# Full-width shapes for a few odd products in a two-layer hybrid decoder trunk

## The chip, the cores and the metric

The kernel runs on one core of a Trainium2 chip. The metric is the device time of one execution in microseconds, as the median of several runs. A core has a matrix engine (TensorE, PE in the profile; its weight loads have a row of their own, PEld), a vector engine (VectorE, DVE), a scalar engine (ScalarE, ACT), a general engine (GpSimd, POOL) and an engine that issues transfers (SyncE, SP). All of them run their own instruction streams and wait for each other by semaphores. Matrix results land in PSUM and are moved from there to SBUF by ScalarE or VectorE.

## What is computed

512 tokens and 16 learned ones (528 rows of 1024 features) go through two layers. Cut to what matters:

```python
def reference(x, meta_tokens, ...):
    h = concatenate([meta, x], axis=1)                     # 528 x 1024
    for i in range(2):
        m = _mixer(_rmsnorm(h, pre_mix_norm[i]), ...)
        h = h + _rmsnorm(m, post_mix_norm[i])
        f = _conv_ffn(_rmsnorm(h, pre_ffn_norm[i]), ...)
        h = h + _rmsnorm(f, post_ffn_norm[i])
    return h[:, 16:]

def _mixer(h, ...):
    rq, rk, rv, rg, gq, gk, gv, gr, ga = split(h @ w_in)   # ga: 16 columns, the rank projection
    o_ret = group_norm(retention(rope(rq), rope(rk), rv)) * silu(rg)        # 4 heads
    log_a = log_sigmoid(ga @ gla_gate_w2 + gla_gate_b) / 16
    o_gla = rms_norm(gated_linear_attention(gq, gk, gv, log_a)) * silu(gr)  # 4 heads
    return concatenate([o_ret, o_gla]) @ w_out

def _conv_ffn(h, ...):
    a, g = split(causal_conv3(h @ ffn_up))
    return (gelu(a) * g) @ ffn_down
```

## The kernel before

Features stand on the 128 partitions, tokens along the free dimension. The 528 tokens are cut in two halves for the projections, 0 to 232 and 232 to 528 (`SPLIT`), and in chunks of 128, 128, 128, 128 and 16 (`CHUNKS`) for attention. Each large product runs in f16 as three matmuls per block of 128 features (`product`, L282 to L284): weights and inputs are split in a high and a low f16 part, and high x high, high x low and low x high are summed. A weight block is loaded as f32 (tile `st`), and ScalarE (L86) and VectorE (L87) make its two parts (tile `unit`); `fetch` does that ten blocks ahead. Small products (scores, states, norms, transposes) run in f32, two PE instructions each, a transpose in one.

The rank projection (`project_rank`, L445) has 16 weight columns. Its unit holds high and low part side by side, twice, 64 columns in all, so two matmuls per block of features do (one for each part of the input), and the sum over the parts falls to the following product with `w2`, in which the gate weights are repeated to match. ScalarE and VectorE fill each of the two copies on their own (the loop in `fetch`). `gate_logits` (L607) multiplies rows 0 to 31 and 32 to 63 of that result with `w2`, first for tokens 0 to 232, then for the rest.

Retention handles four blocks of 128 tokens and a last one of 16: `ret_scores` multiplies 16 key columns with 16 query columns (L565, tile `rst`), masks them (tile `dgrt`), and `head_out` multiplies them with the last 16 rows of v (L499), after the product of the 16 queries with the state (L497), into the same PSUM tile.

A norm over features needs a sum over partitions: `token_rstd` multiplies squares with a column of ones (L230, `nst`), takes the power -1/2 on GpSimd (L215), and spreads the result over the partitions by a diagonal (L236 on VectorE, `ndg`) times ones (L237, `nbc`). It does so in equal groups of at most 128 tokens: two for the first half, four of 74 for the 296 tokens of the second.

The first input is normed otherwise, token by token before its transpose. `start` does so for the first two chunks. For the others, `first_xh` takes squares per row, scales the rows (L378, tile `yt`), transposes them (L361) and evicts them as high and low part, on ScalarE (L363) and VectorE (L364). Apart from that, `raw_h` transposes the unscaled rows (L394) and ScalarE copies them (L395) into the residual `h`.

The order of the work has two sources. `start` fixes the order of ScalarE, VectorE and SyncE by hand. All else is put in order by a planner, which places each engine's instructions by costs of its own; the program only gives the dependencies and a rough order: `mixer` runs the projections of the first seven tiles (`LEAD`) on the first half, then on the second, then tile by tile, and after each one it takes two steps (`tick`) of the background generators in `bg`: the first input's second part (`self.later`), gains, constants, raw transposes and the heads. At layer 1's start, and between mixer and feed-forward part, the norms of the second half run while PE works on the first.

Of the kernel before, what the change touches and what calls it, by code (L numbers as in the profile page):

```python
# [14 lines left out]
P = 128  # L15
# [45 lines left out]
class Block:  # L61
# [10 lines left out]
    def fetch(self):  # L72
        if self.unit is not None:
            return
        nc = self.kern.nc
        if self.st is None:
            self.load()
        st = self.st
        if self.w < 64:
            self.unit = self.kern.wpool.tile([P, self.nk, 2, 2, self.w], F16, tag="unit", name="unit")  # L80
            us = [self.unit[:, :, j].rearrange("p k i c -> p i k c") for j in range(2)]
        else:
            self.unit = self.kern.wpool.tile([P, 2, self.nk, self.w], F16, tag="unit", name="unit")
            us = [self.unit]
        for u in us:
            nc.scalar.activation(u[:, 0], st, AF.Copy, scale=SW)  # L86
            nc.vector.scalar_tensor_tensor(out=u[:, 1], in0=st, scalar=SW, in1=u[:, 0], op0=ALU.mult, op1=ALU.subtract)  # L87


class Kern:  # L90
# [105 lines left out]
    def tables(self):  # L196
# [3 lines left out]
        self.tri = self.g([P, P], F32, "tri")  # L200
# [21 lines left out]
    def token_rstd(self, acc, n0, n1, out):  # L222
# [6 lines left out]
        for i in range(nk):  # L229
            nc.tensor.matmul(st[:w, i : i + 1], acc[:, i * w : (i + 1) * w], self.ones[:, :1], start=True, stop=True)  # L230
# [3 lines left out]
        for i in range(nk):  # L234
# [15 lines left out]
    def norms(self, m, acc, xh, n0, n1, rpost, rpre):  # L250
# [18 lines left out]
        bc = out[1]  # L269
        for k in range(KD):  # L270
            t = self.sm([P, WN], "tmp")
            nc.vector.scalar_tensor_tensor(out=t[:, :n], in0=self.h[:, k, n0:n1], scalar=self.pars[:, rpre + k : rpre + k + 1],
                                           in1=bc[:, :n], op0=ALU.mult, op1=ALU.mult)
            self.split(xh[k], t[:, :n], n0, n1)
# [92 lines left out]
    def first_xh(self, t0, t1, n0, n1):  # L367

        nc = self.nc
        ys = []  # L370
        for t in range(t0, t1):
            w = CHUNKS[t][1]
            y = [self.g([P, 512], F32, "yt") for _ in range(2)]
# [653 lines left out]
```

## Time and profile before

| | us |
|---|---|
| median of 3 runs | 1290.46 (1289.42 to 1291.12) |
| the profiled execution, whole | 1289.08 |
| its span, first to last instruction | 1287.3 |
| mean granted clock of TensorE, share of full speed | 0.993 |
| PE busy in the span | 1259.2 |
| VectorE busy | 738.2 |
| ScalarE busy | 605.6 |
| GpSimd busy | 169.2 |

Times inside the profile count from the span's start. An engine is busy while at least one of its instructions is under way. The chain that ended last is followed back from the last instruction, at each step to what released it.

### The profile page before, as it was taken

What the parts mean: (1) busy time and instruction counts of PE and PEld (TensorE: products, weight loads), DVE (VectorE), ACT (ScalarE), POOL (GpSimd) and SP (SyncE); (2) the same over time, 40 slices, a digit from 0 to 9 for tenths busy, and PEclk for the clock granted to TensorE, in tenths of its full rate; (3) what the DMA queues carried; (4) which work ended last, traced back from release to release, by engine and by line L of the source; (5) the groups of instructions that cost most, each with busy time, mean ns of one, the idle gap of its engine ahead of it and who ended that gap; (6) DMA issues with size and microseconds to landing.
All of it is one profiled execution on the core that took longest, in us unless ns stands there. A gap on an engine that the chain in (4) does not pass through costs nothing.

```text
span 1287.3 us, 26505 instructions
## 1 busy us (share of the span) xinstructions
PE 1259.2 (98%) x11198; PEld 1022.3 (79%) x11198; DVE 738.2 (57%) x1408; ACT 605.6 (47%) x1165; POOL 169.2 (13%) x256
## 2 busy tenths in 40 slices
PE   8999999999999999999989999999999999999997
PEld 7687888879888888989876778889788888884443
DVE  6478846357876665431475888453769666664211
ACT  6664434354755555432345544443548555553200
POOL 1023210153000000000340223001420000000000
PEclk9999999999999999999998999999999999999999
DMA  9521221231533343232232222221405333223001
GB/s 257 162 83 51 67 76 57 67 99 34 148 115 99 94 125 90 68 102 70 80 106 83 83 67 66 67 66 51 132 11 172 100 105 108 99 99 131 33 19 48
DMA packets 202171, 115.46 MB, mean 90 GB/s; under 512 B 6256, under 2 KB 193700, under 8 KB 202052
## 3 DMA queue, kind: packets, MB, share of 16 engines
q1 hardware_dynamic: 201892, 113.24, 30.0%
q8 instruction: 87, 1.43, 0.4%
q0 software_dynamic: 160, 0.52, 0.1%
q14 instruction: 32, 0.26, 0.1%
HBM read 111.65 MB, written 2.10 MB: 88 GB/s over the span
## 4 chain that ended last, share of the span: by engine, by line
PE 86%; DVE 6%; ACT 3%; POOL 2%; issue 1%; DMA 1%; SPq 1%; DVEq 0%; POOLq 0%; ACTq 0%
PE pu L283 12%; PE pu L284 12%; PE pu L282 12%; PE pj L283 6%; PE pj L282 6%; PE pj L284 6%; PE pd L283 3%; PE pd L284 3%; PE pd L282 3%; PE pl L921 3%; PE pl L919 3%; PE pl L920 3%; PE po L282 2%; PE po L283 2%; PE po L284 2%; DVE unit L87 1%
## 5 line engine op out<-in xcount | busy, mean ns | idle before, releaser
L87 DVE SCALAR_TENSOR_TENSOR unit<-st,unit 128x1024 f16<-128x1024 f32 (+2 forms) x210 | 254.4, 1215 | 304.3 <-ACT unit L86 303.5
L283 PE MATMUL pu<-xh,unit 128*128 128x296 f16 (+2 forms) x1408 | 384.6, 274 | 1.4 <-DVE xh L220 1.4
L284 PE MATMUL pu<-xh,unit 128*128 128x296 f16 (+2 forms) x1408 | 384.8, 274 | 0.0
L282 PE MATMUL pu<-xh,unit 128*128 128x296 f16 (+2 forms) x1408 | 382.7, 274 | 1.1 <-ACT xh L219 1.0
L282 PEld LDWEIGHTS <-unit 128*128 128x128 f16 x2912 | 285.5, 98 | 48.4 <-issue 5.7
L283 PEld LDWEIGHTS <-unit 128*128 128x128 f16 x2912 | 285.7, 98 | 48.0 <-issue 6.5
L284 PEld LDWEIGHTS <-unit 128*128 128x128 f16 x2912 | 285.8, 98 | 44.8 <-issue 3.1
L86 ACT ACTIVATE unit<-st 128x1024 f16<-128x1024 f32 (+2 forms) x210 | 214.7, 1027 | 110.5 <-PE pl L921 38.9
L282 PE MATMUL pj<-xh,unit 128*128 128x296 f16 (+2 forms) x896 | 247.4, 277 | 2.6 <-DVE on L530 1.6
L283 PE MATMUL pj<-xh,unit 128*128 128x296 f16 (+2 forms) x896 | 247.8, 277 | 0.0
L284 PE MATMUL pj<-xh,unit 128*128 128x296 f16 (+2 forms) x896 | 247.5, 277 | 0.0
L838 ACT ACTIVATE u<-pu 128x296 f32<-128x296 f32 (+2 forms) x176 | 66.9, 382 | 175.4 <-PE pu L284 175.4
L283 PE MATMUL pd<-ffa,unit 128*128 128x296 f16 (+1 forms) x352 | 96.8, 276 | 0.0
L282 PE MATMUL pd<-ffa,unit 128*128 128x296 f16 (+1 forms) x352 | 96.8, 276 | 0.0
L284 PE MATMUL pd<-ffa,unit 128*128 128x296 f16 (+1 forms) x352 | 96.6, 276 | 0.0
L215 POOL TENSOR_TENSOR rs_r<-rs_t,mhalf 128x1 f32<-128x1 f32 (+5 forms) x33 | 39.1, 1189 | 322.6 <-DVE rs_t L214 201.7
L284 PE MATMUL po<-merged,unit 128*128 128x296 f16 (+2 forms) x256 | 69.9, 274 | 0.0
L283 PE MATMUL po<-merged,unit 128*128 128x296 f16 (+2 forms) x256 | 69.9, 274 | 0.0
L282 PE MATMUL po<-merged,unit 128*128 128x296 f16 (+2 forms) x256 | 69.6, 274 | 0.0
L824 DVE SCALAR_TENSOR_TENSOR ca<-u,cvec,ca 128x528 f32<-128x528 f32 (+1 forms) x88 | 66.5, 756 | 1.2
L824 DVE SCALAR_TENSOR_TENSOR cg<-u,cvec,cg 128x528 f32<-128x528 f32 (+1 forms) x88 | 66.3, 753 | 1.2 <-ACT cg L821 1.2
L920 PE MATMUL pl<-unit,ffa 128*128 128x512 f16 x176 | 66.7, 379 | 0.0
(193 smaller groups left out, 1431.0 us busy)
## 6 DMA issues: line engine op xcount, KB each, us to landing
st<-in_ffn_up SPq DMA_DIRECT2D x88, 512.0 KB, 3.8
st<-in_w_in SPq DMA_DIRECT2D x56, 512.0 KB, 3.7
st<-in_ffn_down SPq DMA_DIRECT2D x38, 512.0 KB, 3.8
st<-in_w_out SPq DMA_DIRECT2D x16, 512.0 KB, 3.6
st<-in_ffn_down SPq DMA_DIRECT2D x8, 384.0 KB, 3.4
out<-yo SPq DMA_DIRECT2D x8, 256.0 KB, 2.1
xt<-in_x SPq DMA_DIRECT2D x6, 256.0 KB, 4.4
cosT<-in_c_cos SPq DMA_DIRECT2D x2, 264.0 KB, 7.7
```

The lines of the kernel that those rows point to most:

```text
L86: nc.scalar.activation(u[:, 0], st, AF.Copy, scale=SW)
L87: nc.vector.scalar_tensor_tensor(out=u[:, 1], in0=st, scalar=SW, in1=u[:, 0], op0=ALU.mult, op1=ALU.subtract)
L215: nc.gpsimd.tensor_tensor(out=r[:w, :n], in0=t[:w, :n], in1=self.mhalf[:w, :n], op=ALU.pow)
L282: nc.tensor.matmul(ps[:, :n], w[:, 0, kk, :], x[:, 0, n0:n1], start=i == 0, stop=False)
L283: nc.tensor.matmul(ps[:, :n], w[:, 0, kk, :], x[:, 1, n0:n1], start=False, stop=False)
L284: nc.tensor.matmul(ps[:, :n], w[:, 1, kk, :], x[:, 0, n0:n1], start=False, stop=i == tot - 1)
L824: nc.vector.scalar_tensor_tensor(out=c[:, lo:L], in0=u[:, i + lo : i + L], scalar=self.cvec[:, ci(i) : ci(i) + 1], in1=c[:, lo:L], op0=ALU ...
L838: nc.scalar.activation(u[:, 2 + n0 : 2 + n1], ps[:, : n1 - n0], AF.Copy, scale=IXW)
L919: nc.tensor.matmul(ps, xa, u[:, 0, k % 2, :], start=k == 0, stop=False)
L920: nc.tensor.matmul(ps, xa, u[:, 1, k % 2, :], start=False, stop=False)
L921: nc.tensor.matmul(ps, xb, u[:, 0, k % 2, :], start=False, stop=k == KF - 1)
```

## The change

It has four parts, each with what its neighbours need.

- The rank unit holds its two parts four times, 128 columns. ScalarE and VectorE fill one copy, GpSimd copies it three times. The projection writes 128 rows. `w2` is loaded into 128 rows by eight transfers, and `gate_logits` uses one group of 32 rows for each pair of weight half and token half, all four products ahead of the evictions.
- The last retention block works on 128 keys (tokens 400 to 528) instead of 16: the score product has 128 key columns, the mask `tri` gets 16 further columns that drop the 112 keys too many, v's last transpose keeps 128 rows, and the decay table follows. The product with v has 128 rows.
- The first input's second part takes its transposes from `raw_h`: the raw rows are transposed, copied to `h`, and scaled there by the norm that is spread over the partitions (`spread`) and the gain, and split (`scaled`, which `norms` now calls too). Scaled rows and their transposes go for these chunks; `first_part` still serves the first two. `raw_h` is called for the first two chunks apart.
- `token_rstd` takes the fewest groups of at most 128 tokens, the last one overlapping where they don't divide: 296 tokens in three groups of 99.

```diff
 class Block: fetch
-        if self.w < 64:
-            self.unit = self.kern.wpool.tile([P, self.nk, 2, 2, self.w], F16, tag="unit", name="unit")
-            us = [self.unit[:, :, j].rearrange("p k i c -> p i k c") for j in range(2)]
+        if self.w < P:
+            self.unit = self.kern.wpool.tile([P, self.nk, P // (2 * self.w), 2, self.w], F16, tag="unit", name="unit")
+            u = self.unit[:, :, 0].rearrange("p k i c -> p i k c")
...
+        if self.w < P:
+            for j in range(1, self.unit.shape[2]):
+                nc.gpsimd.tensor_copy(out=self.unit[:, :, j], in_=self.unit[:, :, 0])

 token_rstd
-        nk = next(i for i in range(1, 9) if n % i == 0 and n // i <= P)
-        w = n // nk
+        nk = -(-n // P)
+        w = -(-n // nk)
+        at = [min(i * w, n - w) for i in range(nk)]
...
-            dg = self.sm([P, P], "ndg")
-            nc.vector.tensor_scalar(out=dg[:w, :w], in0=self.ident[:w, :w], scalar1=r[:w, i : i + 1], scalar2=None, op0=ALU.mult)
-            nc.tensor.matmul(bc[:, i * w : (i + 1) * w], self.ones[:w, :], dg[:w, :w], start=True, stop=True)
+            self.spread(bc[:, c0 : c0 + w], r[:w, i : i + 1], w)

 first_xh
-        ys = []
+        rs = []
         for t in range(t0, t1):
...
-            for i in range(2):
-                nc.vector.tensor_scalar(out=y[i][:w], in0=self.xs[t][i][:w], scalar1=r[:w, 0:1], scalar2=None, op0=ALU.mult)
+            self.squares(t, [self.g([P, 512], F32, "yt") for _ in range(2)])
+            rs.append(self.row_rstd(t))
             yield
+        yield from self.raw_h(t0, t1, n0, n1)
+        bc = self.mx([P, WN], "nbc")
+        for t, r in zip(range(t0, t1), rs):
+            c0, w = CHUNKS[t]
+            self.spread(bc[:, c0 - n0 : c0 - n0 + w], r[:w, 0:1], w)
+        yield from self.scaled(bc, self.xh, n0, n1, R_PRE)
...
+    def spread(self, out, r, w):
+        nc = self.nc
+        dg = self.sm([P, P], "ndg")
+        nc.vector.tensor_scalar(out=dg[:w, :w], in0=self.ident[:w, :w], scalar1=r, scalar2=None, op0=ALU.mult)
+        nc.tensor.matmul(out, self.ones[:w, :], dg[:w, :w], start=True, stop=True)
+
+    def scaled(self, bc, xh, n0, n1, rpre):
+        nc = self.nc
+        n = n1 - n0
         for k in range(KD):
-            self.first_part(k, ys, t0, t1, n0, n1)
+            t = self.sm([P, WN], "tmp")
+            nc.vector.scalar_tensor_tensor(out=t[:, :n], in0=self.h[:, k, n0:n1], scalar=self.pars[:, rpre + k : rpre + k + 1],
+                                           in1=bc[:, :n], op0=ALU.mult, op1=ALU.mult)
+            self.split(xh[k], t[:, :n], n0, n1)
             if k % 2:
                 yield

 project_rank
-                nc.tensor.matmul(ps[:64, :n], u[:, k].rearrange("p j i c -> p (j i c)"), self.xh[k][:, i, n0:n1], start=k + i == 0, stop=k + i == KD)
+                nc.tensor.matmul(ps[:, :n], u[:, k].rearrange("p j i c -> p (j i c)"), self.xh[k][:, i, n0:n1], start=k + i == 0, stop=k + i == KD)

 v_natural
+        w = 16 if ret is None else P
+        vnt = self.sm([w, P], "vnt", bufs=6)
...
+        nc.tensor.transpose(pt2[:w, :], vt[:, L - w : L], self.ident)

 ret_scores
-        nc.tensor.matmul(pst[:16, :], kT[:, 512:528], qT[:, 512:528], start=True, stop=True)
+        nc.tensor.matmul(pst, kT[:, L - P : L], qT[:, 512:528], start=True, stop=True)
...
+        nc.vector.tensor_tensor(out=dt, in0=pst, in1=self.tri[:, P:], op=ALU.mult)

 gate_logits
+        parts = [(pr, n0, n1, self.mx([P, WN], "z")) for n0, n1 in ((0, SPLIT), (SPLIT, L)) for pr in range(2)]
+        for i, (pr, n0, n1, z) in enumerate(parts):
+            rows = slice(32 * i, 32 * i + 32)
+            nc.tensor.matmul(z[:, : n1 - n0], self.w2[rows, pr * P : (pr + 1) * P], gaT[rows, n0:n1], start=True, stop=True)

 mixer
-        gaT = self.g([64, L], F32, "gaT")
-        self.w2 = self.g([64, 256], F32, "w2")
-        for i in range(4):
+        gaT = self.g([P, L], F32, "gaT")
+        self.w2 = self.g([P, 256], F32, "w2")
+        for i in range(8):
             nc.sync.dma_start(self.w2[16 * i : 16 * (i + 1), :], self.a["gla_gate_w2"][l])
```

## Rows read from the trace of the kernel before

**Rows 1.** The page: busy time, share of the span and instructions of each engine, and the chain that ended last by engine.

```profile
PE 1259.2 (98%) x11198; PEld 1022.3 (79%) x11198; DVE 738.2 (57%) x1408; ACT 605.6 (47%) x1165; POOL 169.2 (13%) x256
...
PE 86%; DVE 6%; ACT 3%; POOL 2%; issue 1%; DMA 1%; SPq 1%; DVEq 0%; POOLq 0%; ACTq 0%
```

**Rows 2.** Busy time of each engine in one stretch at layer 1's start: the stretch, its length, PE, PEld, DVE, ACT and POOL busy with their instructions, granted clock, DMA share, GB/s.

```profile
675.10:685.20 10.10, 8.29 (x31) 4.49 (x32) 7.69 (x21) 4.32 (x10) 0.28 (x1) 0.50 0.01 2
```

**Rows 3.** The rank projection (L445): all its matmuls (shortest, median and longest in ns, first and last start), and PE's timeline around two of its groups, one with 232 columns and one with 296: start, duration, line, tiles, weights, input, count.

```profile
L445 PE MATMUL pj<-xh,unit x64: 259/287/456, 13.4 to 689.4; 128*64 128x232 f16 x32, 128*64 128x296 f16 x32
...
660.59 0.26 PE L284 MATMUL pj<-xh,unit 128*128 128x232 f16 x1
660.69 0.26 PE L282 MATMUL pj<-xh,unit 128*128 128x232 f16 x1
660.88 0.39 PE L445 MATMUL pj<-xh,unit 128*64 128x232 f16 x2
661.20 0.27 PE L283 MATMUL pj<-xh,unit 128*128 128x232 f16 x1
...
689.36 0.31 PE L445 MATMUL pj<-xh,unit 128*64 128x296 f16 x1
689.61 0.30 PE L282 MATMUL pj<-xh,unit 128*128 128x296 f16 x1
689.74 0.29 PE L283 MATMUL pj<-xh,unit 128*128 128x296 f16 x1
```

**Rows 4.** PE's timeline where the first input's second part is transposed (L361 scaled rows, L394 raw rows) and where its first rank matmul starts; in brackets the idle time before an instruction and what ended it.

```profile
32.88 1.94 PE L361 MATMUL ptx<-ident,yt 128*128 128x128 f32 x18
35.09 0.29 PE L445 MATMUL pj<-xh,unit 128*64 128x296 f16 x1 [0.27 <-ACT xh L363]
...
48.09 2.13 PE L394 MATMUL pth<-ident,xt 128*128 128x128 f32 x12
```

**Rows 5.** PE's timeline around the two products of a norm in four groups: the sums (L230) with the instruction behind them, and the spread (L237) with the instruction behind it.

```profile
294.90 0.63 PE L230 MATMUL nst<-ones,acc 128*74 128x1 f32 x8
295.39 0.26 PE L283 MATMUL pu<-xh,unit 128*128 128x232 f16 x1
...
663.29 1.03 PE L237 MATMUL nbc<-ndg,ones 74*128 74x74 f32 x8
664.16 0.26 PE L282 MATMUL pj<-xh,unit 128*128 128x218 f16 x1
```

**Rows 6.** What scales and splits: the timelines of VectorE and GpSimd at the start (a conversion that waited, the scaled rows, the evictions; the row norms' power), and the groups by line and shape (count, busy us, mean ns, idle before) of the same work in the later norms and of the raw copies.

```profile
28.22 1.23 DVE L87 SCALAR_TENSOR_TENSOR unit<-st,unit 128x1024 f16<-128x1024 f32 x1 [1.27 <-ACT unit L86]
...
31.82 2.45 DVE L378 TENSOR_SCALAR yt<-xt,rs_r 128x512 f32<-128x512 f32 x6
...
35.33 3.43 DVE L364 SCALAR_TENSOR_TENSOR xh<-ptx,pars,xh 128x272 f16<-128x272 f32 x8
...
29.66 3.47 POOL L215 TENSOR_TENSOR rs_r<-rs_t,mhalf 128x1 f32<-128x1 f32 x3 [18.36 <-DVE rs_t L214]
...
L272 DVE SCALAR_TENSOR_TENSOR tmp<-h,pars,nbc 128x296 f32<-128x296 f32 x24 | 11.1, 515 | 4.9 <-PE nbc L237 4.9
L220 DVE TENSOR_TENSOR xh<-tmp,xh 128x296 f16<-128x296 f32 x24 | 9.8, 457 | 0.0
...
L395 ACT ACTIVATE h<-pth 128x272 f32<-128x272 f32 x8 | 3.1, 399 | 2.5 <-PE pth L394 2.1
```

**Rows 7.** The queues at the start: SyncE's issues of the gate weights, the first two row norms on GpSimd, the conversion of the last unit that the first halves need (VectorE), the eviction behind that tile's last matmul (ScalarE), and GpSimd's only cast (by line and shape).

```profile
15.45 2.43 SPq L713 DMA_DIRECT2D w<-in_gla_gate_w  x3
...
9.83 1.46 POOL L215 TENSOR_TENSOR rs_r<-rs_t,mhalf 128x1 f32<-128x1 f32 x2 [8.71 <-DVE rs_t L214]
...
25.07 1.21 DVE L87 SCALAR_TENSOR_TENSOR unit<-st,unit 128x1024 f16<-128x1024 f32 x1
...
33.08 0.37 ACT L726 ACTIVATE gv<-pj 128x232 f32<-128x232 f32 x1 [0.66 <-PE pj L284]
...
L191 POOL CAST mask<-maskf 128x448 uint8<-128x448 f32 x1 | 1.0, 955 | 1.7 <-DMA maskf<-in_c_mask 1.7
```

**Rows 8.** PE's timeline around layer 0's gate logits.

```profile
58.67 1.16 PE L607 MATMUL z<-gaT,w 32*128 32x232 f32 x8
59.76 0.30 PE L282 MATMUL pj<-xh,unit 128*128 128x296 f16 x1
```

**Rows 9.** PE's timeline around the last block of one retention head's output and the scores of another head.

```profile
173.54 0.39 PE L499 MATMUL o<-vnt,dgrt 16*16 16x128 f32 x2
173.85 1.16 PE L564 MATMUL rs<-rq,rk 128*128 128x128 f32 x8
174.94 0.21 PE L565 MATMUL rst<-rq,rk 128*16 128x16 f32 x2
175.09 0.66 PE L477 MATMUL ptk<-ident,rk 128*128 128x128 f32 x4
```

**Rows 10.** Layer 1's start: PE's last projection before its wait and the first one after it, and VectorE's diagonals and first scaling in the norms that PE waits for.

```profile
671.90 0.26 PE L284 MATMUL pj<-xh,unit 128*128 128x232 f16 x1
...
680.15 0.41 PE L445 MATMUL pj<-xh,unit 128*64 128x296 f16 x1 [1.10 <-ACT xh L219]
...
660.33 0.76 DVE L236 TENSOR_SCALAR ndg<-ident,rs_r 74x74 f32<-74x74 f32 x4 [1.12 <-POOL rs_r L215]
...
664.36 2.74 DVE L261 SCALAR_TENSOR_TENSOR tmp<-m,par,nbc 128x296 f32<-128x296 f32 x6 [3.27 <-PE nbc L237]
```

More of the change, by code (lines that the diff above doesn't have):

```diff
@@ L78, in fetch @@
         st = self.st
-        if self.w < 64:
-            self.unit = self.kern.wpool.tile([P, self.nk, 2, 2, self.w], F16, tag="unit", name="unit")
-            us = [self.unit[:, :, j].rearrange("p k i c -> p i k c") for j in range(2)]
-        else:
[L83 to L87, printed above, removed]
+        if self.w < P:
+            self.unit = self.kern.wpool.tile([P, self.nk, P // (2 * self.w), 2, self.w], F16, tag="unit", name="unit")
+            u = self.unit[:, :, 0].rearrange("p k i c -> p i k c")
+        else:
+            u = self.unit = self.kern.wpool.tile([P, 2, self.nk, self.w], F16, tag="unit", name="unit")
+        nc.scalar.activation(u[:, 0], st, AF.Copy, scale=SW)
+        nc.vector.scalar_tensor_tensor(out=u[:, 1], in0=st, scalar=SW, in1=u[:, 0], op0=ALU.mult, op1=ALU.subtract)
+        if self.w < P:
+            for j in range(1, self.unit.shape[2]):
+                nc.gpsimd.tensor_copy(out=self.unit[:, :, j], in_=self.unit[:, :, 0])
 class Kern:
@@ L225, in token_rstd @@
         n = n1 - n0
-        nk = next(i for i in range(1, 9) if n % i == 0 and n // i <= P)
-        w = n // nk
+        nk = -(-n // P)
+        w = -(-n // nk)
+        at = [min(i * w, n - w) for i in range(nk)]
         st = self.mx([P, 8], "nst")
-        for i in range(nk):
-            nc.tensor.matmul(st[:w, i : i + 1], acc[:, i * w : (i + 1) * w], self.ones[:, :1], start=True, stop=True)
+        for i, c0 in enumerate(at):
+            nc.tensor.matmul(st[:w, i : i + 1], acc[:, c0 : c0 + w], self.ones[:, :1], start=True, stop=True)
         r = self.rstd(st[:w, :nk], nk, 1.0 / D, EPS, w)
@@ L268, in norms @@
         yield from self.token_rstd(acc2, n0, n1, out)
[L269 to L274, printed above, removed]
+        yield from self.scaled(out[1], xh, n0, n1, rpre)
     def product(self, ps, units, rhs, n0, n1):
@@ L386, in raw_h @@
         nc = self.nc
[L387 to L395 removed]
+        for k in range(KD):
+            pt = self.mx([P, WN], "pth")
+            for t in range(t0, t1):
+                c0, w = CHUNKS[t]
+                nc.tensor.transpose(pt[:, c0 - n0 : c0 - n0 + w], self.xs[t][k // 4][:w, k % 4 * P : (k % 4 + 1) * P], self.ident[:w, :w])
+            nc.scalar.activation(self.h[:, k, n0:n1], pt[:, : n1 - n0], AF.Copy)
+            if k % 2:
+                yield
@@ L467, in v_natural @@
                 nc.scalar.activation(vn[:, j, :], pt[:, j, :], AF.Copy, scale=up[:, j : j + 1])
-            nc.scalar.activation(vnt, pt2[:16, :], AF.Copy, scale=up[:16, 4:5])
+            nc.scalar.activation(vnt, pt2, AF.Copy, scale=up[:, 4:5])
         return lambda j: vn[:, j, :] if j < 4 else vnt
@@ L560, in ret_scores @@
         dg = self.g([P, 4, P], F32, "dgr")
-        dt = self.sm([16, 16], "dgrt", bufs=4)
+        dt = self.sm([P, 16], "dgrt", bufs=4)
         ps, pst = self.mx([P, 4, P], "rs"), self.mx([P, 16], "rst")
@@ L963, in run @@
         self.later = self.first_xh(2, 5, HALF, L)
-        for gen in (self.later, self.gains(), self.mixer_constants(), self.raw_h()):
+        for gen in (self.later, self.gains(), self.mixer_constants(), self.raw_h(0, 2, 0, HALF)):
             self.spawn(gen)
```

50 lines of the change are left out of this document (15 added, 35 removed).

## The prediction

> **What bounds the kernel now.** I read the page's busy line and chain first [rows 1]: TensorE (PE) is busy 98% of the span and carries 86% of the chain that ended last. So a change here is worth what it takes off PE's stream, plus what it takes off the few stretches where PE waits. The granted clock by stretch comes next [rows 2]: around 680 us, at layer 1's start, it is 0.50, the lower of its two levels (1.2 GHz), after a wait. A busy PE hides its pace, because each matmul's record overlaps the next one's, so I read starts, not durations: in [rows 3] a 232-column f16 matmul follows the last one after 0.10 us, a 296-column one after 0.13. Whatever exceeds these steps is what an odd shape costs.
>
> **The rank projection.** It uses 64 columns of the array, its neighbours 128. In [rows 3], 660.69 to 660.88 is a step of 0.19 into the 64-column form where 0.10 is usual, and the two rank matmuls take 0.32 (660.88 to 661.20) where two usual ones take 0.20. With 296 columns one takes 0.25, not 0.13. So each group of rank matmuls costs 0.09 going in and 0.12 inside and going out, 0.21 together, however many matmuls it holds. The 64 matmuls stand in 37 groups in PE's order (10, 9, 10, 8 by layer and half), between 13.4 and 689.4. 37 x 0.21 is 7.8; a few groups follow a wait or an odd transpose, which leaves 2.0, 1.6, 2.1 and 1.9 us, **7.6 us** together. At 128 columns they take the usual step, since the f16 neighbours load 128 columns at it already. The planner may group them otherwise; without a change of form a group costs nothing.
>
> **The first input's second part.** Removed: 24 transposes of scaled rows (L361). 18 of them take 1.94 us from 32.88 [rows 4], 24 by the same pace 2.6, and 0.3 for the 16-row ones that stand apart: 2.9 us of PE, with 0.7 of wait for xh between 34.8 and 35.9. The raw transposes (L394) exist before and after; 12 take 2.13 us from 48.09, 0.17 each with the 16-row ones among them and the last one's tail left out, so 24 take 4.1 us. They only move ahead, because they need no row scale. Added on PE: three products with ones, two instructions each. One of 74 columns takes 0.11 (663.29 to 664.16 for eight [rows 5]), so six take 0.65 to 0.8; I take 0.75. Net **3.6 - 0.75 = 2.9 us** less.
> On VectorE six scalings and eight evictions go, 2.45 + 3.43 = 5.9 us [rows 6]; eight scalings by the spread norm and eight subtractions come, (0.515 + 0.457) x 272/296 = 0.89 us for each k, 7.1 us. PE can use 1.0 us of matmuls for each k (two rank and two times three, at 0.126), so 0.89 still feeds it. The first xh stands where it did: the last of three row norms leaves GpSimd at 33.1 (29.66 + 3.47), then a diagonal (0.2), the spread (0.4), a scaling (0.48) and a copy (0.4) give 34.6 to 35, against the wait that ends at 35.09 now [rows 4].
>
> **Friction at the start**, bounded from both sides. SyncE issues four more loads of the gate weights; three take 2.43 us [rows 7], so four take 0 (in SyncE's gaps) to 3.2 us ahead of the weight loads behind them. The last unit that the first halves need is converted by 26.3 (25.07 + 1.21); its tile's last matmul ends at 33.1, so with 24 steps of 0.10 the first starts near 30.7: 4.4 us of cover. GpSimd copies the rank unit three times, 256 elements each: by the nearest row, a cast of 448 in 0.955 us [rows 7], 0.55 each (0.1 to 0.96 as bounds). They stand behind two row norms that end at 11.3, so the unit is whole at 12.9 (at worst 14.2), and PE's first rank matmul starts at 13.4; ScalarE and VectorE each lose one of two conversions in return. ScalarE takes the eight raw copies (0.40 each [rows 6]) some 10 us sooner, among unit conversions and PSUM evictions. Bounds for all three: 0 to 4 us; I take **1.5 us**, the lower half, since each has cover of its own.
>
> **The gate logits.** Eight instructions in two row groups take 58.67 to 59.76, 1.09 us [rows 8]. In four row groups both halves run at once, two passes of the longer half with one weight load ahead: about 0.65, **0.45 us** less in layer 0 (0 to 0.55). In layer 1 the first half's four run apart while PE waits, and I give nothing there (0 to 1.0).
>
> **The last retention block.** The product of vnt and dgrt goes from 16 x 16 to 128 x 16, the form of the product ahead of it. Its two instructions take 0.31 us (173.54 to 173.85 [rows 9]) where an f32 step without a change of form is 0.11; of the changes of form one goes, 0.10 us, eight heads: **0.8 us**. The short score block goes from 16 to 128 weight columns; before, the step into it is 0.2 or a little more (the eight ahead take 173.85 to 174.94, 1.09, not 0.88) and the two take 0.15 (174.94 to 175.09). Eight f32 loads of 74 columns take 0.49 (294.90 to 295.39 [rows 5]), 0.067 a step; in proportion 128 columns set 0.11, so 0.11 + 0.22 = 0.33 stands against 0.35: **0.2 us** for eight (-0.4 to 0.8). The wider transposes of v change no step.
> The Trainium skill (TensorE: Matmul & The Clock Gate, LDWEIGHTS) speaks against this part: a weight load takes its columns divided by 1.2 ns, so 16 to 128 columns would cost 94 ns more for each of 16 instructions, 1.5 us lost, and the sum would be smaller by 1.7 us. The f32 rows agree with its slope (0.067 us for 74 columns [rows 5]); what it leaves out is the change of form that goes with the narrow load, which the rows price at about as much.
>
> **Fewer norm groups.** 296 tokens in three groups, not four: the spread's eight instructions (0.87 us [rows 5]) become six, 0.65; the sums' eight (0.49) become six longer ones, 0.47. 0.23 us a call, and 0.19 of VectorE for one diagonal less [rows 10]. Four calls lie in PE's stream: **0.9 us**.
>
> **Layer 1's start.** Here PE's savings meet a wait: PE runs dry at 672 and is fed at 680.15 [rows 10]. The chain behind that begins with the spread at 663.29: VectorE waited 3.27 us for it, though its diagonals are ready at 661.1 (660.33 + 0.76); it merely stands behind PE's earlier matmuls. The first ten rank groups lie ahead of it, so 1.8 of their 2.1 us (the rest becomes wait for xh) bring the chain forward, and PE is fed that much sooner. One norm call saves 0.23, the one at half clock 0.43; the eight rank groups after the wait save 1.9. Together **4.3 us**.
>
> **Sum.** Start: 2.0 + 1.6 + 2.9 + 0.45 - 1.5 = 5.4; retention 1.0; norms 0.9; layer 1's start 4.3: 11.6 us. The profiled execution took 1289.1 us (span 1287.3 and 1.8 around it), 1.4 below the median of the runs. 1289.1 - 11.6 = 1277.5, on the median's footing 1279 us.
>
> **Rivals.**
> - Feed rules the start: ScalarE's raw copies and VectorE's 0.89 us a k leave PE waiting, and the start gives nothing. For it: VectorE sat idle 1.27 us for a ScalarE conversion at 28.22 [rows 6]. Against: PE has raw transposes as filler. 1279 + 5.4 = 1284.
> - Layer 1's wait stays where it is, because the order puts the spread no sooner: 2 to 4 us lost, 1283.
> - That wait shrinks so far that the clock doesn't fall: 10.1 us at half clock [rows 2] are worth up to 5.0 us, 1274. Against: 8 us of wait less 2 is still long.
> - Wash: the planner orders PE's stream anew around the smaller pieces and gives the gain back in waits; 1289.
> - **Slower**, one mechanism: the eight raw copies (3.2 us) go ahead of the conversion on which VectorE waits at 28.22, and the norms queue behind that on VectorE. The three row norms end at 33.1 + 3.2 = 36.3, xh comes at 38.1; PE, which ends the first half at 33.1 - 2.0 + 4.1 = 35.2, waits 3 us, a wait like the one that stands ahead of the low clock in layer 1. The low clock decides: without it this is only the first rival; with it the start's 5.4 are gone, and 5.0 for as long a stretch at half clock and 3 of wait come on top (6, if the loads of the gate weights hold up that conversion by their 3.2 too): 1279 + 13.4 to 16.4 = 1292 to 1295, 1294 as one number.
>
> **Chances.** Forecast 0.55 (1275 to 1283 by its own bounds), feed 0.13, layer 1's wait 0.12, clock kept 0.06, wash 0.08, slower 0.06. The range 1273 to 1287 leaves out the wash, the slower case and a tail of the others. A measurement of this kernel tells about 0.2%, 2.6 us, from no change: faster 0.86 (the first four), same 0.08, slower 0.06.
>
> **What would show it.** Right: no step of 0.19 or 0.32 around the rank matmuls; the gate logits of layer 0 in about 0.65 us and 5 to 7 us sooner than 58.67; the spread at 663.29 some 8 us sooner, PE fed some 9 us sooner than 680.15; the distances between later stages unchanged. Wrong: PE idle between the halves at 33 to 42 us, a granted clock of 0.50 there, or a wait in layer 1 that is longer by what PE saved ahead of it.

## The result and the profile after

The changed kernel takes **1276.03 us** (median of 4 runs, 1275.50 to 1277.14), the kernel before 1290.15 beside it (4 runs, 1289.42 to 1291.12): ratio 0.9891, 95% interval 0.9874 to 0.9908. The forecast was 1279.0, its range 1273 to 1287. The profiled execution took 1276.04 us, with a span of 1274.3 (before: 1287.3).

A table of starts on PE says where the time went. Each number is the start in us of the first or last matmul of that name in the profiled execution; "half clock" lists the stretches near layer 1's start with a granted clock of 0.50. The runs e1 to e12 are explained below; the row of e9_neither is an execution 1.6 us under that run's median.

| kernel | median | first z, layer 0 | first pu, layer 0 | last pd, layer 0 | last z, layer 1 | last pl | half clock |
|---|---|---|---|---|---|---|---|
| before | 1290.15 | 58.67 | 290.24 | 651.54 | 698.63 | 1279.54 | 675.0-685.3 |
| after | 1276.03 | 53.16 | 284.13 | 644.96 | 687.56 | 1267.06 | 668.2-675.0 |
| e1_rank64 | 1283.83 | 57.97 | 288.89 | 649.71 | 695.52 | 1274.85 | 674.4-681.2 |
| e2_first | 1283.44 | 58.12 | 290.29 | 651.13 | 695.03 | 1274.45 | 673.0-683.2 |
| e3_ret | 1277.64 | 52.75 | 284.19 | 645.01 | 688.66 | 1268.65 | 666.3-676.6 |
| e4_norm | 1277.34 | 52.98 | 283.76 | 645.05 | 689.42 | 1269.40 | 667.1-677.3 |
| e5_before_grouped | 1298.08 | 63.27 | 295.06 | 656.35 | 707.84 | 1288.77 | 661.0-667.8, 688.3-695.2 |
| e6_after_grouped | 1288.67 | 58.21 | 288.95 | 649.79 | 700.56 | 1280.06 | 654.3-661.1, 681.6-688.4 |
| e7_logits_two | 1276.34 | 52.90 | 284.07 | 644.90 | 687.90 | 1267.24 | 669.1-675.9 |
| e8_tails | 1278.08 | 55.45 | 287.07 | 647.91 | 691.72 | 1269.53 | 669.6-679.8 |
| e9_neither | 1287.31 | 59.00 | 289.86 | 650.70 | 696.79 | 1276.09 | 675.8-682.7 |
| e10_head_tails | 1272.97 | 52.25 | 281.67 | 642.50 | 686.42 | 1264.22 | 664.4-674.6 |
| e11_fill | 1276.05 | 53.11 | 283.98 | 644.82 | 687.14 | 1266.68 | 671.1-674.5 |
| e12_feed | 1272.82 | 53.02 | 282.25 | 643.08 | 685.80 | 1263.62 | 670.3-673.7 |

Before less after, stage by stage: 5.51 us up to the first z, 0.60 to pu (0.37 in the gate logits and 0.69 in one layer's retention, less 0.5 lost in between), 0.47 to the last pd (two norm calls), 4.49 across layer 1's start, 1.41 to the last pl.

The half clock comes elsewhere too, and not in each execution alike. The changed kernel has it from 12.8 to 16.3, 111.8 to 115.2 and 746.7 to 750.1, the kernel before from 757.0 to 760.4; e1_rank64 from 12.2 to 19.0, e2_first from 10.8 to 14.2 and 116.6 to 120.0, e3_ret from 11.0 to 14.4, e9_neither not at all before 675. Some differences of about 1 us between two rows come from that and not from an edit.

PE is still busy 98% of the span, now 1248.2 us of it (before 1259.2 [rows 1]):

```profile
PE 1248.2 (98%) x11156; PEld 1024.4 (80%) x11156; DVE 737.8 (58%) x1405; ACT 604.7 (47%) x1163; POOL 169.0 (13%) x262
```

**The rank projection**, answering to [rows 3]: the group of all its matmuls, and PE's timeline around a group with 232 and one with 296 columns.

```profile
L455 PE MATMUL pj<-xh,unit x64: 259/289/451, 14.0 to 678.8; 128*128 128x232 f16 x32, 128*128 128x296 f16 x32
...
20.76 0.26 PE L277 MATMUL pj<-xh,unit 128*128 128x232 f16 x1
20.86 0.36 PE L455 MATMUL pj<-xh,unit 128*128 128x232 f16 x2
21.06 0.26 PE L278 MATMUL pj<-xh,unit 128*128 128x232 f16 x1
...
38.23 0.41 PE L455 MATMUL pj<-xh,unit 128*128 128x296 f16 x2
38.48 0.29 PE L278 MATMUL pj<-xh,unit 128*128 128x296 f16 x1
```

The reader compares starts: 0.10 us into the group and 0.20 for its two matmuls (before 0.19 and 0.32), 0.125 each with 296 columns (before 0.25 for one). The first rank matmul starts at 14.0, before at 13.4.

**The start**, answering to [rows 4, 6, 7, 8]: GpSimd's copies of the rank unit and the row norms' power; VectorE's conversion that waits for ScalarE and its first scaling; PE's raw transposes after their only wait between 17 and 59 us, its change to the second half, and the gate logits.

```profile
11.47 2.46 POOL L88 COPY unit<-unit 128x256 f16<-128x256 f16 x3 [1.50 <-DVE unit L85]
28.13 1.57 POOL L216 TENSOR_TENSOR rs_r<-rs_t,mhalf 128x1 f32<-128x1 f32 x3 [14.21 <-DVE rs_t L215]
...
29.75 1.23 DVE L85 SCALAR_TENSOR_TENSOR unit<-st,unit 128x1024 f16<-128x1024 f32 x1 [1.64 <-ACT unit L84]
33.87 1.72 DVE L390 SCALAR_TENSOR_TENSOR tmp<-h,pars,nbc 128x272 f32<-128x272 f32 x4
...
28.27 0.60 PE L402 MATMUL pth<-ident,xt 128*128 128x128 f32 x3 [0.38 <-ACT kq L738]
36.74 0.26 PE L279 MATMUL pj<-xh,unit 128*128 128x232 f16 x1
36.84 0.29 PE L455 MATMUL pj<-xh,unit 128*128 128x296 f16 x1
53.16 0.78 PE L619 MATMUL z<-gaT,w 32*128 32x232 f32 x8
53.88 0.30 PE L277 MATMUL pj<-xh,unit 128*128 128x296 f16 x1
```

The second half's first matmul (36.84) follows the first half's last after the usual 0.10: the wait for xh at 35.09 [rows 4] is gone, with scaling under way since 33.87. The gate logits take 0.72 us (53.16 to 53.88), before 1.09.

**The norm groups and a retention head**, answering to [rows 5, 9]. A norm's sums take 0.47 us, its spread 0.66 (before 0.49 and 0.87).

```profile
288.79 0.60 PE L232 MATMUL nst<-ones,acc 128*99 128x1 f32 x6
289.26 0.26 PE L278 MATMUL pu<-xh,unit 128*128 128x232 f16 x1
...
655.26 0.82 PE L382 MATMUL nbc<-ndg,ones 99*128 99x99 f32 x6
655.92 0.26 PE L277 MATMUL pj<-xh,unit 128*128 128x218 f16 x1
...
167.69 0.39 PE L510 MATMUL o<-sn,rq 128*16 128x128 f32 x2
167.91 0.38 PE L512 MATMUL o<-vnt,dgrt 128*16 128x128 f32 x2
168.23 1.16 PE L577 MATMUL rs<-rq,rk 128*128 128x128 f32 x8
169.22 0.29 PE L578 MATMUL rst<-rq,rk 128*128 128x16 f32 x2
```

From o<-vnt to rs it is 0.32, as before (0.31); what is gone lies ahead of it, 0.22 from o<-sn (in e3_ret, which has the old form, 0.32). From rs to rst 0.99, before 1.09.

**Layer 1's start**, answering to [rows 2, 10]: PE's timeline, then windows (columns as in [rows 2]).

```profile
665.20 0.66 PE L232 MATMUL nst<-ones,acc 128*99 128x1 f32 x6 [1.27 <-DVE acc L248]
667.44 0.43 PE L382 MATMUL nbc<-ndg,ones 99*128 99x99 f32 x2 [1.58 <-DVE ndg L381]
667.80 0.79 PE L619 MATMUL z<-gaT,w 32*128 32x232 f32 x4
668.53 1.17 PE L382 MATMUL nbc<-ndg,ones 99*128 99x99 f32 x4
670.90 0.40 PE L455 MATMUL pj<-xh,unit 128*128 128x296 f16 x1 [1.20 <-ACT xh L220]
```

```profile
670.00:672.00 2.00, 1.10 (x4) 0.55 (x4) 2.00 (x6) 1.60 (x4) 0.00 (x0) 0.50 0.00 0
672.00:674.00 2.00, 1.95 (x9) 1.13 (x8) 2.00 (x7) 0.60 (x2) 0.00 (x0) 0.50 0.03 8
```

The spread that stood at 663.29 stands at 655.26, 8.0 us sooner; PE is fed at 670.90, before at 680.15, 9.25 sooner. The wait has moved along and not vanished. In both windows the clock is at 0.50 and VectorE is busy without a gap, while PE in the first of them, up to 670.90, is not; e11_fill shows what that means.

### The profile page after: what moved, and what is told of

It reads as the page before. It is cut to its first block, busy times and chain, and to the rows that moved or that the text cites. A ratio compares the mean times of both kernels' runs of the same rounds, so it can differ in the third digit from the quotient of the medians.

```text
span 1274.3 us, 26435 instructions
## 1 busy us (share of the span) xinstructions
PE 1248.2 (98%) x11156; PEld 1024.4 (80%) x11156; DVE 737.8 (58%) x1405; ACT 604.7 (47%) x1163; POOL 169.0 (13%) x262
## 4 chain that ended last, share of the span: by engine, by line
PE 87%; DVE 5%; ACT 2%; POOL 2%; issue 1%; DMA 1%; SPq 1%; DVEq 0%; POOLq 0%; ACTq 0%
PE pu L278 12%; PE pu L279 12%; PE pu L277 12%; PE pj L277 6%; PE pj L278 6%; PE pj L279 6%; PE pd L277 3%; PE pd L278 3%; PE pd L279 3%; PE pl L933 3%; PE pl L932 3%; PE pl L931 3%; PE po L277 1%; PE po L279 1%; PE po L278 1%
## 5 line engine op out<-in xcount | busy, mean ns | idle before, releaser
L216 POOL TENSOR_TENSOR rs_r<-rs_t,mhalf 128x1 f32<-128x1 f32 (+5 forms) x33 | 35.8, 1089 | 313.3 <-DVE rs_t L215 186.1
```

The costliest lines, as they stand in the source:

```text
L216: nc.gpsimd.tensor_tensor(out=r[:w, :n], in0=t[:w, :n], in1=self.mhalf[:w, :n], op=ALU.pow)
```

## The experiments

All were timed beside the kernel before.

**e1_rank64** undoes the rank projection (64 columns, its logits in two row groups); all else stays changed.

```
-    nc.tensor.matmul(ps[:, :n], u[:, k]..., self.xh[k][:, i, n0:n1], ...)
+    nc.tensor.matmul(ps[:64, :n], u[:, k]..., self.xh[k][:, i, n0:n1], ...)
-        gaT = self.g([P, L], F32, "gaT")
+        gaT = self.g([64, L], F32, "gaT")
```

> The changed kernel with the rank projection back at 64 columns (unit filled by ScalarE and VectorE, gate logits in two row groups, four loads of the gate weights). Theory, a price per change of form on PE: 39 groups of rank matmuls stand in PE's order, 0.21 us each, 8.2 us less what falls into waits (about 0.6), and 0.4 for the logits: 8 us over the changed kernel, 1284, ratio to before 0.995. Rival, the gain comes from an order that the planner laid better or from engines freed at the start: within 2 us of the changed kernel, 1278 or less.

Measured: 1283.83 us, ratio to before 0.9961 (0.9948 to 0.9973), 7.8 over the changed kernel: 4.8 up to the first z and 3.2 at layer 1's start. The size came as the theory said, but the 4.8 is not clean: this execution has 6.8 us at half clock in the start, the changed kernel's 3.4.

**e2_first** undoes the first input's second part.

```
-        yield from self.raw_h(t0, t1, n0, n1)
-        bc = self.mx([P, WN], "nbc")
-        ...
-        yield from self.scaled(bc, self.xh, n0, n1, R_PRE)
+        for k in range(KD):
+            self.first_part(k, ys, t0, t1, n0, n1)
```

> The changed kernel with the first input's second part as before (scaled rows, transposed a second time). Theory, PE's stream counts: 24 transposes come back (2.9 us with their waits 3.6) and 0.75 of spread products go: 3 us over the changed kernel, 1279. Rival, the friction that I charged to the start (1.5 us) is due to the raw copies and goes with them: 1.5 us over, 1277.5, or none.

Measured: 1283.44, ratio 0.9954 (0.9942 to 0.9967), 7.4 over the changed kernel. Theory and rival both miss by 4 us or more. The first z stands at 58.12, 0.9 us ahead of e9_neither's, which has neither part, where the rank groups of the start were priced at 3.6. PE's timeline in this run says what took most of the rest:

```profile
27.85 0.26 PE L277 MATMUL pj<-xh,unit 128*128 128x232 f16 x1 [0.70 <-ACT kq L742]
31.75 0.26 PE L277 MATMUL pj<-xh,unit 128*128 128x232 f16 x1 [1.37 <-ACT kq L742]
```

With the faster rank projection PE reaches its next tile before ScalarE has emptied a PSUM buffer (kq). The kernel before, whose PE was slower, has no such wait between 17 and 35 us. The first pu stands at 290.29, where the kernel before has it. The last of the gain goes between 110 and 154 us: this execution is at half clock from 116.6 to 120.0, e9_neither's is not, and a lead of 1.1 us becomes a lag of 0.4.

**e9_neither** completes the square: both undone.

```
e1_rank64's edit and e2_first's edit together
```

> Both the rank projection on 128 columns and the first input's new second part are undone; the last retention block on full rows and the fewer norm groups are kept. Undone one at a time they cost 7.8 and 7.4 us over the changed kernel's 1276.0. Theory (the start's gain is joint: each of the two parts alone runs into PE's waits between the first input's halves, and only both together give it; taken back together they cost no more than the start's 5.5 and layer 1's 3.2 to 4): 1276 + 5.5 + 3.2 to 4 = 1285 to 1286, and seen from the other side the kernel before (1289.5) less the 1.6 of the retention and the 1.3 of the norms = 1286.6. Rival (the two parts are independent and their prices add up): 1276 + 7.8 + 7.4 = 1291.2, slower than before. The products with the gate logits stand near 58.4 by the theory, against 53.2 in the changed kernel.

Measured: 1287.31 (10 runs), ratio 0.9980 (0.9970 to 0.9989): 0.7 above the joint theory (1285 to 1286.6), 3.9 below the additive rival (1291.2), which falls. By medians it is 11.3 us from neither to both; alone, the first input's part gives 3.5 (e1_rank64) and the rank projection 3.9 (e2_first). At the first z it is 5.8 from neither to both (59.00 to 53.16), and 1.0 (57.97) and 0.9 (58.12) alone. Either way 3.9 us come only with both.

Part of that is the clock. The windows from 13 to 20 us, first e9_neither, then e1_rank64 (columns as in [rows 2]):

```profile
13.00:20.00 7.00, 6.34 (x45) 3.83 (x45) 5.06 (x10) 5.03 (x10) 0.00 (x0) 1.00 1.17 288
```

```profile
13.00:20.00 7.00, 7.00 (x34) 3.89 (x32) 5.17 (x10) 5.03 (x10) 0.00 (x0) 0.57 1.09 284
```

From its first 128-column projection matmul to its 25th e1_rank64 takes 7.72 us (14.80 to 22.52), e9_neither 5.55 (14.19 to 19.74). With these 2.2 us counted out, as an estimate, the first input's part alone gives 3.2 at the first z, and 1.7 come only with both. That is as much as e2_first's waits for kq (2.07) exceed the changed kernel's (0.38). **So between 1.7 and 3.9 of the 5.8 us come only with both.** Whether e1_rank64's order brings its clock down at the start, or only this execution had it, one trace of it can't tell.

**e3_ret** undoes the last retention block.

```
-        nc.tensor.matmul(pst, kT[:, L - P : L], qT[:, 512:528], ...)
+        nc.tensor.matmul(pst[:16, :], kT[:, 512:528], qT[:, 512:528], ...)
-        vnt = self.sm([w, P], "vnt", bufs=6)
+        vnt = self.sm([16, P], "vnt", bufs=6)
```

> The changed kernel with the last retention block as before (16 keys). Theory: one change of form more for each of eight heads and the narrow score block: 1.0 us over, 1277. Rival, the 128 column load costs what its 112 further columns take (0.09 us for each of 16 instructions): 0.7 us under the changed kernel, 1275.3.

Measured: 1277.64, ratio 0.9911 (0.9896 to 0.9927), 1.6 over. This interval overlaps the changed kernel's (0.9874 to 0.9908), as e4_norm's does, so the stages have to show it. From the first z to pu it takes 0.47 more, from layer 1's last z to the end 0.49: 0.96 together, as the theory said. But in these stages the changed kernel's execution loses 0.2 us twice to half clock (from 111.8 and 746.7), and e3_ret has none there. Behind those stretches, up to the first po of each layer, e3_ret takes 0.69 and 0.68 more: 1.4 us is what the retention block is worth. The rest of the 1.6 is layer 1's start with a longer stretch at half clock (10.2 for 6.8 us).

**e4_norm** puts the norms back to four groups of 74 columns.

```
-        nk = -(-n // P)
-        w = -(-n // nk)
+        nk = next(i for i in range(1, 9) if n % i == 0 and n // i <= P)
+        w = n // nk
```

> The changed kernel with 296 tokens in four norm groups. Theory: 0.23 us for each of four calls in PE's stream, 0.23 and 0.43 in the chain of layer 1's start and a fourth diagonal there: 1.7 us over, 1277.7. Rival, the norms' time lies beside other work: 0.

Measured: 1277.34, ratio 0.9910 (0.9897 to 0.9924), 1.3 over; 0.46 from pu to the last pd, two calls. As forecast.

**e5_before_grouped, e6_after_grouped**: is the rank projection's price paid per change of array form or per 64-column matmul? In both kernels its loop runs from the last k and the second half of xh to the first. The scheduler then gathers the 64 rank matmuls into 7 groups (before: 37) and 4 groups, so that changes of form go while matmuls stay.

```
-        for k in range(KD):
-            for i in range(2):
+        for k in reversed(range(KD)):
+            for i in (1, 0):
```

> The kernel before with the rank projection's sum over features taken from the last block to the first: the same 64 matmuls with the same 64 column loads, but all their inputs are there when the first one can run, so they stand in 7 groups, not 37. Theory, the price is per change of form: 30 groups less at 0.21 us, 6.3 us, of which up to 2 go to waits where rank matmuls filled in: 1284 to 1286, ratio 0.996. Rival, a 64 column load is slow by itself, once for each matmul: no gain, 1290 or slower.

> The changed kernel with the same reversed sum, 4 groups at 128 columns. Theory: no change of form to save, so only the order's own effect is left, 0 to 2 us over the changed kernel: 1276 to 1278. Rival, grouping itself helps: 1272.

Measured: 1298.08, ratio 1.0064 (1.0050 to 1.0078), and 1288.67, ratio 0.9989 (0.9980 to 0.9998). As times both miss the theory, by 12 and by 10 us or more, and the first lies on the rival's side: a rank projection that starts with the last k waits for the last xh, which neither theory nor rival had. From e6_after_grouped:

```profile
654.43 1.12 PE L232 MATMUL nst<-ones,acc 128*99 128x1 f32 x6 [4.36 <-DVE acc L248]
656.84 3.25 PE L455 MATMUL pj<-xh,unit 128*128 128x232 f16 x16 [1.28 <-DVE xh L221]
```

The question is still answered by the steps. A group of nine 64-column matmuls in e5_before_grouped:

```profile
45.09 0.65 PE L394 MATMUL pth<-ident,xt 128*128 128x128 f32 x4
45.67 1.32 PE L445 MATMUL pj<-xh,unit 128*64 128x296 f16 x9
46.92 0.44 PE L394 MATMUL pth<-ident,xt 128*128 128x128 f32 x2
```

45.67 to 46.92 is 1.25 us for nine; at 0.126 each, the step of the 128-column form, nine take 1.13. So the narrow weights cost nothing for each matmul; the group pays 0.12 once, besides the step into it. At full clock that is shown with 296 columns alone: the long groups with 232 are at half clock in both runs, and step 0.193 with 64 columns as with 128. Between these two kernels the change is worth 9.4 us, ungrouped 14.1: 4.7 less, as far as two orders with such waits can be compared. The Trainium skill (TensorEngine Tiling (Array Packing), Key Properties) says that changing the tiling mode drains TensorE; the longer steps at each change agree with it and add the price, though what TensorE does in them the trace doesn't show.

**e7_logits_two** keeps the 128-column rank projection and puts the logits into two row groups.

```
-            rows = slice(32 * i, 32 * i + 32)
+            rows = slice(32 * (i % 2), 32 * (i % 2) + 32)
```

> The changed kernel with all gate logits in rows 0 to 63, two row groups. Theory: 1.09 us for layer 0's logits instead of 0.71, 0.4 us over the changed kernel, 1276.4, too little for the times and to be read from the profile. Rival, the four groups do more (shorter chain behind the logits): over 1 us.

Measured: 1276.34, ratio 0.9894, 0.3 over the changed kernel: too little to tell in the medians, plain in the trace, 1.10 us instead of 0.72:

```profile
52.90 1.16 PE L619 MATMUL z<-gaT,w 32*128 32x232 f32 x8
54.00 0.30 PE L277 MATMUL pj<-xh,unit 128*128 128x296 f16 x1
```

**e8_tails, e10_head_tails**: if each odd form costs, the 16-row transposes should go too. e8_tails runs those of the first input and of the heads' outputs on 128 rows padded with zeros, e10_head_tails those of the outputs alone (16 of them):

```
-    nc.tensor.transpose(pt[:, c0 - n0 : c0 - n0 + w], ... ont, self.ident[:w, :w])
+    nc.tensor.transpose(pt[:, c0 - n0 : c0 - n0 + P], ... ont, self.ident)
```

> The changed kernel carried on: the transposes of the 16 row tails (raw x and head outputs) run on 128 rows, filled with zeros by GpSimd, their 112 further columns left unused. Theory: 24 transposes at 0.36 us of two steps become 0.22, 0.145 each, 3.5 us less than the changed kernel: 1272.5, ratio 0.9865. Rival, the zero fill and the waits for it take it back: 1276.

> The changed kernel with only the 16-row transposes of the heads' outputs on full 128 rows (16 of them, the padding is zeros); the first input keeps its 16-row tails. Theory (price of the change of array form: 0.20 in and 0.16 out against 0.11 for a full one, about 0.14 each; the loss that the version with the first input's tails had was in the start, by its longer copies and its order): the start as in the changed kernel (first gate logits at 53.2), attention of layer 1 shorter by 1.0 to 1.7, that of layer 0 by as much: 2.3 us less, 1273.7. Rival (the order built anew around them costs as much as they bring): 1275.5 to 1276.5.

Measured: 1278.08, ratio 0.9907 (0.9894 to 0.9921), a miss, and **1272.97**, ratio 0.9868 (0.9854 to 0.9881), 3.1 below the changed kernel, a hit. In both, layer 1 from its first d to its first po takes 170.1 us instead of 171.8; in e10_head_tails layer 0 takes 171.6 instead of 173.2, so 16 transposes brought 3.2 us, 0.20 each where 0.14 was expected. The steps between PE's starts explain it: the step into each went from 0.20 to 0.11 and the one out of it from 0.16 to 0.11, the expected 0.14; and where an f32 product stands behind (6 of 16), its second step went from 0.21 to 0.11 too. These three steps give 3.06 us together. Layer 1's start gave 1.3 of it back (43.92 us from the last pd to the last z, 42.60 in the changed kernel), with a longer stretch at half clock. The first z came 0.9 sooner, of which 0.8 is a transfer that landed earlier; so the hit is in part luck.

e8_tails loses 2.3 at the start (first z at 55.45), where its raw transposes wait for ScalarE to empty their buffers, and its layer 0 takes 173.9, with a wait of 1.89 us for ScalarE at 122.7 and half clock from 123.4 to 126.8. Longer copies, which the expectation of e10_head_tails names, are hardly the reason: the raw copies of 272 columns take 395 ns, in the changed kernel 374. The waits at the start:

```profile
25.10 0.88 PE L405 MATMUL pth<-ident,xt 128*128 128x128 f32 x6 [1.05 <-ACT h L406]
...
30.37 0.26 PE L277 MATMUL pj<-xh,unit 128*128 128x232 f16 x1 [1.36 <-ACT h L406]
```

**e11_fill** adds three f32 products with no use, where PE waits 1.58 us in layer 1's start; PE's order is else the same.

```
+            wu = self.mx([P, WN], "warm2")
+            for _ in range(3):
+                nc.tensor.matmul(wu[:, :n], self.ones, acc[:, :n], start=True, stop=True)
         r = self.rstd(...)
```

> The changed kernel with three f32 products of ones with acc (128 x 296, their result unused) put behind the sums of squares of layer 1's last norm, where PE waits 1.58 us for the diagonals; PE's order is otherwise the same. Three take about 3 x 0.5 = 1.5 us. Theory (the stretch of 6.8 us at the lower clock from 668.2 follows the two waits of 1.27 and 1.58 us, and with the second one filled it doesn't come): 6.8 / 2 = 3.4 us less, 1272.6, and the granted clock at layer 1's start stays 1.00. Rival (one wait of 1.27 and one of 1.2 are enough to bring the clock down, or the fill holds up the diagonals' products): 1276 to 1276.5, with a stretch at 0.50 between 664 and 685.

Measured: 1276.05, ratio 0.9891 (0.9876 to 0.9906): nothing. Half of the theory's mechanism came: the clock stays at 1.00 up to 671.1, and half clock lasts 3.4 us, not 6.8. The gain did not: PE starts the second half at 670.26 at full pace, and is at its next xh too early.

```profile
670.26 0.29 PE L459 MATMUL pj<-xh,unit 128*128 128x296 f16 x1 [1.32 <-ACT xh L220]
670.39 0.54 PE L281 MATMUL pj<-xh,unit 128*128 128x296 f16 x3
671.82 0.65 PE L459 MATMUL pj<-xh,unit 128*128 128x296 f16 x2 [0.90 <-DVE xh L221]
```

The last z of layer 1 comes 0.42 us sooner (687.14), 0.28 of it across layer 1's start. Halving the time at the lower clock ought to give 1.7 (3.4 us at half pace). PE was 0.64 ahead at 670.26, and the wait of 0.90 for VectorE's xh, which the changed kernel doesn't have, took more than half of that back. From 671.82 PE runs on without a wait, at half pace up to 674.5; what those 2.7 us cost was not tried.

**e12_feed** acts on that: e10_head_tails with the fill, and in that norm half of VectorE's subtractions on GpSimd.

```
-        self.nc.vector.tensor_tensor(out=dst[:, 1, n0:n1], ...)
+        (self.nc.gpsimd if pool else self.nc.vector).tensor_tensor(out=dst[:, 1, n0:n1], ...)
```

> The version with the heads' 16-row transposes on full rows (1273.0), with the three filling products of ones with acc in layer 1's start, and in that one norm four of the eight subtractions that make the second half of xh on GpSimd, not VectorE; else the same order. Theory (what bounds layer 1's start once PE is fed is VectorE, which scales and subtracts without a gap for 7 us while PE waits 0.90 us for xh and runs part of that time at the lower clock for nothing lost): VectorE does 4 x 0.40 = 1.6 us less in that stretch, GpSimd's four take about 0.85 each beside it, so the last xh comes 0.6 to 1.3 us sooner; with the 0.4 that the fill alone gave, 1.0 to 1.7 us less: 1271.6, between 1271.3 and 1272. Rival (the feed isn't the bound: only the fill's 0.4 shows): 1272.6. Second rival (GpSimd's slower subtraction is late and PE waits for it): 1273 or more, with a wait for GpSimd's xh in front of a rank matmul.

Measured: 1272.82, ratio 0.9867 (0.9850 to 0.9883), the same as e10_head_tails: a miss, nearest to the rival's 1272.6. Groups by line in layer 1's start (count, busy us, mean ns, idle before), first e11_fill, then e12_feed on VectorE and on GpSimd, and the timelines of these two:

```profile
L221 DVE TENSOR_TENSOR xh<-tmp,xh 128x296 f16<-128x296 f32 x8 | 3.2, 458 | 0.0
```

```profile
L221 DVE TENSOR_TENSOR xh<-tmp,xh 128x296 f16<-128x296 f32 x4 | 3.2, 829 | 0.0
```

```profile
L221 POOL TENSOR_TENSOR xh<-tmp,xh 128x296 f16<-128x296 f32 x4 | 3.1, 774 | 5.9 <-ACT xh L220 5.6
```

```profile
669.57 1.40 DVE L221 TENSOR_TENSOR xh<-tmp,xh 128x296 f16<-128x296 f32 x2
...
672.62 1.77 DVE L221 TENSOR_TENSOR xh<-tmp,xh 128x296 f16<-128x296 f32 x2
```

```profile
668.97 1.67 POOL L221 TENSOR_TENSOR xh<-tmp,xh 128x296 f16<-128x296 f32 x2 [3.88 <-ACT xh L220]
672.39 1.67 POOL L221 TENSOR_TENSOR xh<-tmp,xh 128x296 f16<-128x296 f32 x2 [1.75 <-ACT xh L220]
```

VectorE does half as many subtractions in the same 3.2 us, because each takes 829 ns beside GpSimd's and not 458. The scalings and subtractions last 6.9 us in both runs, from 669.21 to 676.14 and from 667.47 to 674.39. Nothing was taken off the feed, so the theory that a lighter feed brings 0.6 to 1.3 was not tried by this run. That layer 1's start is 1.2 us shorter than in e10_head_tails (42.72 for 43.92) fits the fill alone: there half clock began at 664.4, ahead of the norm's products, where no feed hides it. The times don't show it because e12_feed's execution reached its first z 0.8 us later (53.02 for 52.25).

## Why the prediction was right

The likeliest case came, 3 us faster than its number and inside its own bounds of 1275 to 1283. Term by term (forecast, then measured):

- **Start 5.4, measured 5.9** (5.51 up to the first z, 0.37 in the logits), but not as its parts were laid out. 2.0 + 1.6 for rank groups, 2.9 for the transposes, 0.45 for logits and -1.5 for friction were added as if each stood alone. e9_neither and its neighbours show that the rank groups' 3.6 don't: with the old transposes they give 0.9 at the first z, because 2.07 us turn into waits for kq. The new first input alone gives 1.0 there, or 3.2 by the estimate without the low clock. The sum came out because both parts were in the change, and in part by luck, since the friction was a choice between 0 and 4. The step that failed is the sentence "Whatever exceeds these steps is what an odd shape costs": it is a price on PE's stream, and PE's stream was the limit at the start only as long as the feed was faster.
- **The copies on GpSimd**: 0.82 us each (2.46 for three), not 0.55, inside the bounds of 0.1 to 0.96. The unit is whole at 13.9, and PE waits 0.44 us for it and starts its first rank matmul at 14.0; before, it started at 13.4 behind a wait for xh. The friction was real, and small.
- **The slower rival**: its first half is seen. ScalarE is full between 27 and 34 us, VectorE waits 1.64 for a conversion (1.27 before). But the spread was so early that scaling began at 33.87 and PE came at 36.84: 3 us of cover, no wait between the halves, and a granted clock of 1.00 there. Part of the cover is the power on GpSimd, 1.57 us for three row norms where 3.47 was taken over.
- **Gate logits 0.45, measured 0.37** (1.09 to 0.72).
- **Retention 1.0, measured 1.4**, both between e3_ret and the changed kernel and between the kernel before and it (0.69 in layer 0, 0.67 in layer 1); e3_ret's stages show 0.96 because of the clock. The split was off: the scores were given 0.2, and their steps give 0.10 per head, 0.8 for eight, the upper bound. The output gives the 0.8 it was given. Of these 1.6 some 0.3 shows up again as a longer step behind rst, by 0.14 in one head of each layer. The rule of the Trainium skill that was set against this part (TensorE: Matmul & The Clock Gate, LDWEIGHTS; by the prediction's estimate from it, a load of 128 columns costs 94 ns more than one of 16) would have made the part a loss of 0.7 us. The trace shows a step of 0.11 into rst with 128 columns, but the step into the 16-column form that it replaces was 0.20.
- **Norms 0.9, measured 0.21 + 0.02 a call** as forecast; e4_norm gives 0.46 for two.
- **Layer 1's start 4.3, measured 4.5.** The chain moved as worked out (8.0 us sooner for the spread, 9.25 for the feed). The half-clock stretch is 6.8 us where 10.2 stood, which the forecast's sum did not have.
- **"Clock kept" at up to 5.0 us** was mis-sized. e11_fill took 3.4 us off the stretch and got 0.3 across layer 1's start; e12_feed, with 6.8 us less than e10_head_tails, got 1.2. That is 0.1 to 0.2 for each us, not a half, because part of what PE gains comes back as a wait for VectorE's xh (0.90 in e11_fill). How much the remaining 3.4 us hide was not tried.
- **What is left**: the forecast on the profiled footing was 1277.5, the profiled execution took 1276.0. 0.5 of the 1.5 lies in the start, 0.4 in retention, 0.2 at layer 1's start, 0.3 between layer 1's heads and its feed-forward part, and 0.5 behind the last pl. Against that stand 0.5 lost in layer 0: 0.2 just behind the logits, 0.3 at half clock from 111.8.

The four parts undone one at a time cost 7.8 + 7.4 + 1.6 + 1.3 = 18.1 us against 14.1 for all. The 4.0 between them match the 3.9 that e9_neither shows by its median: undoing one part of a change measures that part given the others, and these sums need not close.

## What to carry to other kernels

Look for the odd array forms in a matmul stream by the distance between starts, and count groups, not instructions: one group costs the same whatever its length. Before adding such prices up, ask for each stretch how far the next engine's feed is behind; two parts that lighten PE and its feed can be worth more together than alone, here by 1.7 to 3.9 of 5.8 us. Before reading a difference of 1 us as the price of an edit, compare the granted clock of the two executions up to there. When the last odd form is cheap to pad (16 rows of a tile that is filled with zeros), pad it where PE doesn't stand close behind another engine: the same padding gained 3.2 us at the heads, and at the start the first z came 2.3 later with it.

## What the runs showed of the hardware

- **Change of array form**: about 0.09 us into a 64-column group of f16 matmuls and 0.12 inside it and out of it, paid once per group, of one matmul or of many (e5_before_grouped). A 16-row f32 transpose among full ones costs 0.09 going in and 0.05 going out, and 0.10 more at the second step of an f32 product behind it (e10_head_tails).
- **VectorE beside GpSimd**: a subtraction of two SBUF tiles of 128 x 296 takes 458 ns alone and 829 ns while GpSimd does the same. The Trainium skill (SBUF — State Buffer, SBUF: two separate sides) says that the two engines take turns at one port pair, each for a whole instruction, when VectorE has two SBUF inputs; the trace agrees: each of VectorE's four ends 0.32 us after the GpSimd subtraction that was under way when it began (670.04, 670.97, 673.46 and 674.39 against 669.72, 670.64, 673.14 and 674.07).
- **Low clock under a feed**: 3.4 us less at half clock gave 0.3 us (e11_fill), 6.8 us less 1.2 (e12_feed beside e10_head_tails).
- **Run to run**: the same start gave its first z at 53.16 in the changed kernel and at 52.25 in e10_head_tails, with the same order up to there. PE waited for the same transfer up to 10.68 in the one and 9.88 in the other, which is 0.8 of it; the half clock from 12.8 to 16.3, which only the first has, left little. So 0.9 us at the first z tell nothing of an edit.
